# RWKV preparation: TensorE in program order, one tapped projection between keys and receptances, projection parts in front of each key score

## The chip, the cores and the metric

The kernel runs on one core of a Trainium2 chip. The metric is the time of one execution in device microseconds (us). Five engines work side by side, each through its own queue in order: TensorE (PE, matmuls; PEld, its weight loads), VectorE (DVE), ScalarE (ACT), GpSimd (POOL) and the sync engine (SP), which issues DMAs here. ScalarE and GpSimd issue DMAs too.

## What is computed

One layer of a trunk with two token mixers on the same input, 128 context and 1024 latent tokens (T = 1152), width 1024. A single projection `w_in` gives the receptances, keys and values of the RWKV mixer (each 512 wide, 4 blocks of 128 columns), its decay and rate inputs, the query, key, value, output and gate columns of the mLSTM mixer, and the merge gates. The part that matters here, of the RWKV mixer:

```
decay = exp(-DECAY_SCALE * sigmoid(w0 + einsum(tanh(wd), w_up)))      # per direction
a = sigmoid(a0 + einsum(ad, a_up))                                    # per direction
kk = k * kk_scale ;  kk = kk / max(norm(kk, per head), 1e-12)
k_dir = k * (1 + (a - 1) * k_a)
# per token: S = S*w - (S kk)(kk a)^T + v k^T ;  y = S r  (forward and backward)
bonus = sum(r * k_dir * r_k) * v
```

The scan over tokens is worked in chunks of 64 tokens. For a chunk, products of keys with decays (KR, BK) give a 64x64 triangular system for each head; its inverse (the "solve") is made before the scan. The mLSTM queries and keys get a 3x3 convolution over the latent grid ("taps") and SiLU.

## The kernel before

A projection of 128 columns (`gemm_block`, line 389) loads its weights (issued by ScalarE), splits them into a high and a low part (`split_w`, line 353: ScalarE line 367, VectorE line 368), and runs three parts of 384 tokens (`gemm_part`); a part is 24 matmuls (3 products of halves x 8 slices of the depth) into one of three large PSUM buffers, and an evacuation by ScalarE. `zr_block` (line 419) adds the token shift of the RWKV columns (`zr_shift`, four VectorE instructions, lines 414 and 416). `zm_qk` (line 578) is a tapped projection: after its evacuation VectorE runs 10 instructions of `conv_taps` (lines 47 and 50), then SiLU and a write to memory. `zm_o`, `zm_v`, `zm_gates` and `zg` are untapped.

The preparation is the loop of four passes p from line 603, one for two heads each. A pass projects keys (kt), receptances (rt) and values (vt), and makes the norm of the keys: squares, the matmul `ptss` with a block of ones (line 627), its evacuation on VectorE (line 628), Ln and Exp on ScalarE, line 631. Then for each direction d: rate matmuls `ptw` and `pta` (lines 642 and 646) with Sigmoid evacuations into the single tiles cs and at, and three groups g of 6 chunks. A group has a running sum on VectorE (line 653 or 655), two Exp on ScalarE, some nine VectorE instructions that fill the tiles KR and BK (two buffers each), four writes to memory by sync, and the key score `ptA` (line 690, 12 matmuls of 64x64, seen as 24 records), which needs lines 667, 669 or 671, and 677. ScalarE evacuates the score into Am (line 691), and after three groups four DMAs write it to Ad. ptss, ptw, pta, ptA and the transposes share five small PSUM buffers. After both directions come the transposes of the values and the bonus (line 720).

`solve` (line 506) works on an engine of its own choice: it loads Ad, runs 31 steps of two instructions (lines 526 and 528) and writes Xnd and Xtd. GpSimd runs five solves, called in passes 1 to 3; VectorE runs the sixth, at the end of pass 3. The scan behind line 725 loads KR, BK, Xtd (tile TT) and Xnd (tile XN) of its first chunks, and starts with the scores `psc` (line 850) and the merge `pmh`, `pmt` (lines 874 and 883).

The order within each engine is drawn up before the run by a planner, from the program's order, from costs of its own, and from free buffers; an engine can so take a later step early. An instruction issued by an `Ordered` engine while its switch `on` is set keeps program order on that engine. In the preparation no switch was set. FILL (line 598) lists the mLSTM and gate projections that follow each direction's work: the first of a pass stands behind direction 0, the others at the end of the pass, and the planner moved their parts between the scores.

## Time and profile before

| | |
|---|---|
| median of 3 runs | 2254.72 us (2248.45 to 2261.33) |
| the profiled execution | 2242.87 us, span of its instructions 2241.2 us |
| granted TensorE clock, mean | 0.972 |
| busy: PE, DVE, ACT, POOL | 2097.6, 1379.5, 820.4, 566.2 us |
| preparation, first ptss to first psc | 131.94 to 619.18 us |

The trace can be asked in several views: busy time by stretch, groups of instructions by line, the timeline of one engine or of all, and the waits. Times of the trace are microseconds from the span's start. "Idle before" is the engine's time without work just before an instruction, and behind the arrow stands what ended it. A busy TensorE is not TensorE at its peak, as its matmuls overlap; its work is better counted by the distance between starts.

### The profile page before, as it was taken

What the parts mean: (1) busy time and instruction counts of PE and PEld (TensorE: products, weight loads), DVE (VectorE), ACT (ScalarE), POOL (GpSimd) and SP (SyncE); (2) the same over time, 40 slices, a digit from 0 to 9 for tenths busy, and PEclk for the clock granted to TensorE, in tenths of its full rate; (3) what the DMA queues carried; (4) which work ended last, traced back from release to release, by engine and by line L of the source; (5) the groups of instructions that cost most, each with busy time, mean ns of one, the idle gap of its engine ahead of it and who ended that gap; (6) DMA issues with size and microseconds to landing.
All of it is one profiled execution on the core that took longest, in us unless ns stands there. A gap on an engine that the chain in (4) does not pass through costs nothing. (4 is left out here: it accounts for less than half of the span.)

```text
span 2241.2 us, 39749 instructions
## 1 busy us (share of the span) xinstructions
PE 2097.6 (94%) x16323; PEld 1936.2 (86%) x16323; DVE 1379.5 (62%) x2155; ACT 820.4 (37%) x1611; POOL 566.2 (25%) x727
## 2 busy tenths in 40 slices
PE   6999998998889989979889999999999999999996
PEld 4998998988878878878888878999999999999995
DVE  4766777879655566654743465645656665566558
ACT  3664746363134433346421244432221222212213
POOL 2000198888722324255312111000000000000004
PEclk8999999999989999989999999999999999999999
DMA  9134443645645655377676531211111021111104
GB/s 267 54 89 124 117 129 99 164 108 137 167 134 129 158 135 127 109 221 235 193 238 203 183 120 69 67 47 40 55 57 48 29 66 51 51 30 57 47 20 169
DMA packets 382453, 254.55 MB, mean 114 GB/s; under 512 B 86305, under 2 KB 357829, under 8 KB 382272
## 3 DMA queue, kind: packets, MB, share of 16 engines
q1 hardware_dynamic: 235232, 139.11, 22.2%
q10 hardware_dynamic: 136912, 88.56, 13.5%
q0 software_dynamic: 10128, 24.35, 4.0%
q8 instruction: 128, 2.10, 0.4%
q14 instruction: 53, 0.43, 0.1%
HBM read 186.73 MB, written 65.23 MB: 112 GB/s over the span
## 5 line engine op out<-in xcount | busy, mean ns | idle before, releaser
L381 PE MATMUL pg<-act,whi 128*128 128x384 f32 (+1 forms) x3808 | 724.7, 337 | 0.5 <-DVE act L344 0.4
L381 PEld LDWEIGHTS pg<-act,whi 128*128 128x128 f32 (+1 forms) x3808 | 665.9, 188 | 12.8 <-DVE act L344 0.8
L381 PE MATMUL pg<-act,wlo 128*128 128x384 f32 (+1 forms) x1904 | 373.0, 336 | 7.8 <-DVE wlo L368 7.8
L381 PEld LDWEIGHTS pg<-act,wlo 128*128 128x128 f32 (+1 forms) x1904 | 332.8, 187 | 11.3 <-DVE wlo L368 8.1
L368 DVE TENSOR_TENSOR wlo<-wraw,whi 128x1024 fp32r<-128x1024 f32 x130 | 165.0, 1270 | 222.1 <-ACT whi L367 221.9
L47 DVE SCALAR_TENSOR_TENSOR ua<-uraw,par,ua 128x945 f32<-128x945 f32 (+2 forms) x176 | 214.7, 1220 | 39.5 <-ACT ua L1516 36.4
L381 PE MATMUL pfd<-whi,f 128*128 128x512 f32 x792 | 227.5, 395 | 6.5 <-DVE facc L1588 6.5
L1590 POOL TENSOR_TENSOR x<-facc,grow 128x512 f32<-128x512 f32 x17 | 24.3, 1452 | 822.7 <-DVE facc L1588 822.7
L367 ACT ACTIVATE whi<-wraw 128x1024 fp32r<-128x1024 f32 x130 | 136.7, 1053 | 166.8 <-PE pg L381 83.8
L381 PEld LDWEIGHTS pfd<-whi,f 128*128 128x128 f32 x792 | 146.4, 188 | 37.2 <-DVE facc L1588 9.1
L1588 DVE TENSOR_TENSOR facc<-pfd,facc 128x512 f32<-128x512 f32 x180 | 122.0, 686 | 52.3 <-PE pfd L381 52.3
L528 POOL TENSOR_TENSOR Lb<-Lb,tmp 96x31 f32<-96x31 f32 (+15 forms) x155 | 129.7, 837 | 12.1
L526 POOL TENSOR_TENSOR tmp<-La,Lb 96x31 f32<-96x31 f32 (+15 forms) x155 | 120.2, 776 | 28.0 <-DMA La<-Ad 16.2
L381 PE MATMUL pfd<-wlo,f 128*128 128x512 f32 x396 | 122.6, 391 | 0.0
L1520 ACT ACTIVATE ua<-ua 128x1152 f32<-128x1152 f32 x22 | 25.7, 1168 | 217.2 <-DVE ua L47 217.2
L69 PE MATMUL pg<-act,whi 128*128 128x384 f32 x496 | 104.3, 362 | 0.0
L1530 ACT ACTIVATE f<-ua 128x384 fp32r<-128x384 f32 x66 | 32.1, 518 | 194.1 <-DVE ua L1529 194.1
L69 PEld LDWEIGHTS pg<-act,whi 128*128 128x128 f32 x496 | 92.1, 203 | 1.1
L1464 PE MATMUL pwo<-whi,act 128*128 128x512 f32 x288 | 90.2, 393 | 1.1 <-ACT whi L367 1.1
L47 DVE SCALAR_TENSOR_TENSOR qacc<-zraw,par,qacc 128x945 f32<-128x945 f32 (+2 forms) x64 | 84.2, 1316 | 9.7 <-ACT qacc L584 9.2
L381 PEld LDWEIGHTS pfd<-wlo,f 128*128 128x128 f32 x396 | 74.3, 188 | 16.8
L860 DVE TENSOR_TENSOR KA<-psc,msk 64x512 f32<-64x512 f32 x72 | 49.2, 684 | 63.8 <-ACT A L859 58.1
(398 smaller groups left out, 3289.8 us busy)
## 6 DMA issues: line engine op xcount, KB each, us to landing
wraw<-in_w_in ACTq DMA_DIRECT2D x44, 512.0 KB
wraw<-in_ffn_up ACTq DMA_DIRECT2D x44, 512.0 KB
zraw<-in_ada_w SPq DMA_DIRECT2D x24, 512.0 KB
wraw<-in_ffn_down ACTq DMA_DIRECT2D x22, 512.0 KB
KRd<-KR SPq DMA_DIRECT2D x24, 384.0 KB
sgz<-zraw ACTq DMA_DIRECT2D x16, 576.0 KB
KA<-KRd SPq DMA_DIRECT2D x72, 128.0 KB
BKs<-BKd SPq DMA_DIRECT2D x36, 256.0 KB
```

The lines of the kernel that those rows point to most:

```text
L47: v.scalar_tensor_tensor(o, img[:, r0 + i:r1 + i, c0 + j:c1 + j], wt, o, op0=ALU.mult, op1=ALU.add)
L69: return (lambda *a, **k: tc.keep_in_program_order(f(*a, **k))) if self.on else f
L367: s.activation(hi, raw, AF.Copy)
L368: v.tensor_tensor(lo, raw, hi.bitcast(F32), op=ALU.subtract)
L381: pe.matmul(out, wt(hw, k), at(ha, k), start=(i == 0), stop=(i == last))
L526: e.tensor_tensor(t3, L[:, j, i].unsqueeze(2).to_broadcast([NI, n, m]), X[:, j:j + 1, c].to_broadcast([NI, n, m]), op=ALU.mult)
L528: e.tensor_tensor(X[:, i, c], X[:, i, c], t3, op=ALU.subtract)
L860: v.tensor_tensor(q.KA[orr, :, h, :], sc_[h][orr], msk[orr, d:d + 1, :].to_broadcast([64, 4, 128]), op=ALU.mult)
L1464: pe.matmul(pts[b][q], AS[g][:, ha, k, 128 * o:128 * o + 128], wo2[k][hw][:, 0, 512 * q:512 * q + 512], start=(k == 0 and i == 0), stop=(k ...
L1520: s.activation(ua, ua, AF.Silu)
L1530: s.activation(f2[:, 0, gs], ua[:, gs], AF.Copy)
L1588: v.tensor_tensor(acc[:, b, qs], pt, acc[:, b, qs], op=ALU.add)
```

## The change

TensorE's switch is set for the preparation, so its instructions keep the program's order there. A projection becomes a generator that stops after each part (a "step"). A pass now projects keys, then one tapped projection, then receptances; the values and the rest of FILL form a chain of steps, and two, two, two, one, two and one of them are issued in front of the six key scores, the others at the end of the pass. The rates of direction 1 are issued behind the first of the two steps in front of direction 0's last score. FILL is reordered so that a tapped projection comes first in each pass. Three small steps of each group go from VectorE to ScalarE: the copies to WL, the copy of the first column of KR, and the scale and bias of kx. The calls of the other fill functions turn into `yield from` in the same manner as the one shown.

```diff
@@ -386,10 +387,16 @@
         mm_split(pt[:ncol], lambda h, k: w2[h][:, k, :], lambda h, k: AS[g][:, h, k, :], nk)
         evac(g, pt)
 
-    def gemm_block(src, evac, nk=8, ncol=128, ps_=None):
+    def gemm_steps(src, evac, nk=8, ncol=128, ps_=None):
+
         w2 = split_w([kp(src)], nk, ncol)
         for g in range(3):
             gemm_part(w2, g, evac, ncol, nk, ps_)
+            yield
+
+    def gemm_block(*a, **k):
+        for _ in gemm_steps(*a, **k):
+            pass
 
     w_in = A["w_in"][0]
 
@@ -416,10 +423,14 @@
             v.scalar_tensor_tensor(dst[:, a:b - 1], raw[:, a + 1:b], hmu[:, i:i + 1], dst[:, a:b - 1],
                                    op0=ALU.mult, op1=ALU.add)
 
+    def zr_steps(i, dst):
+        raw = stage()
+        yield from gemm_steps(w_in[:, 128 * i:128 * i + 128], zr_evac(i, raw, dst))
+        zr_shift(i, raw, dst)
+
     def zr_block(i, dst):
-        raw = stage()
-        gemm_block(w_in[:, 128 * i:128 * i + 128], zr_evac(i, raw, dst))
-        zr_shift(i, raw, dst)
+        for _ in zr_steps(i, dst):
+            pass
 
 
     rows = [mods1(0)]
@@ -565,7 +576,7 @@
 
         def evac(g, pt):
             s.activation(vf[:, G3 * g:G3 * g + G3], pt, AF.Copy)
-        gemm_block(w_in[:, 2944 + 128 * f:3072 + 128 * f], evac)
+        yield from gemm_steps(w_in[:, 2944 + 128 * f:3072 + 128 * f], evac)
         vs = stage()
         for q in range(3):
             pt = pss([128, 3, 128], "ptvm")
@@ -595,11 +606,12 @@
             return [(slice(0, 2), slice(0, 2), -1), (slice(14, 18), slice(2, 6), -1)]
         return [(slice(14 - 6 * g + 0, 20 - 6 * g), slice(0, 6), -1)]
 
-    FILL = [[(zm_o, 0), (zm_qk, 0), (zm_gates, 0), (zm_qk, 1)],
-            [(zm_o, 1), (zm_qk, 2), (zm_v, 0), (zm_qk, 3)],
-            [(zm_o, 2), (zm_qk, 4), (zm_v, 1), (zm_qk, 5)],
-            [(zm_o, 3), (zm_qk, 6), (zm_v, 2), (zm_qk, 7), (zm_v, 3), (zg, 0), (zg, 1), (zg, 2),
-             (zg, 3)]]
+
+    FILL = [[(zm_qk, 0), (zm_o, 0), (zm_gates, 0), (zm_qk, 1)],
+            [(zm_qk, 2), (zm_o, 1), (zm_v, 0), (zm_qk, 3)],
+            [(zm_qk, 4), (zm_o, 2), (zm_v, 1), (zm_qk, 5)],
+            [(zm_qk, 6), (zm_o, 3), (zm_v, 2), (zm_v, 3), (zm_qk, 7), (zg, 0), (zg, 1), (zg, 2), (zg, 3)]]
+    pe.on = True
     for p in range(4):
         pc = slice(128 * p, 128 * p + 128)
         wraw = stage()[:, 0:512]
@@ -613,10 +625,13 @@
         v.tensor_tensor(wup[1], wraw, wup[0].bitcast(F32), op=ALU.subtract)
         kt = pp.tile([128, T], F32, name="kt", tag="kt")
         zr_block(4 + p, kt)
+        fn, f = FILL[p][0]
+        for _ in fn(f):
+            pass
         rt = pp.tile([128, T], F32, name="rt", tag="rt")
         zr_block(p, rt)
         vt = pp.tile([128, T], F32, name="vt", tag="vt")
-        zr_block(8 + p, vt)
+        steps = chain(zr_steps(8 + p, vt), *(fn(f) for fn, f in FILL[p][1:]))
 
         kk = pp.tile([128, T], F32, name="kk", tag="kk")
         sq = pp.tile([128, T], F32, name="sqk", tag="zmisc")
@@ -631,8 +646,7 @@
         v.scalar_tensor_tensor(kk, kt, P("rwkv_kk_scale", p), kk, op0=ALU.mult, op1=ALU.mult)
         kds = pp.tile([128, T], F32, name="kds", tag="kds")
         rf = rst.rearrange("p c t -> p (c t)")
-        for d in range(2):
-            Am = pp.tile([128, NCH, LC], F32, name="Am", tag="zmisc")
+        def rates(d):
             cs_ = pp.tile([128, T], F32, name="cs", tag="cs")
             at_ = pp.tile([128, T], F32, name="at", tag="at")
             for g in range(3):
@@ -645,6 +659,11 @@
                 for i in range(2):
                     pe.matmul(pt, wup[i][:, 2 + d], zad[d][:, gs], start=(i == 0), stop=(i == 1))
                 s.activation(at_[:, gs], pt, AF.Sigmoid, bias=P("rwkv_a0", 4 * d + p))
+            return cs_, at_
+
+        for d in range(2):
+            cs_, at_ = rates(0) if d == 0 else nxt
+            Am = pp.tile([128, NCH, LC], F32, name="Am", tag="zmisc")
             for g in range(3):
                 gs = slice(G3 * g, G3 * g + G3)
                 cg = slice(6 * g, 6 * g + 6)
@@ -662,16 +681,16 @@
                 e0 = LC - 1 if d == 0 else 0
                 f0 = 0 if d == 0 else LC - 1
                 for n, c, st in wl_pos(d, g):
-                    v.tensor_copy(WL[:, n, d, p:p + 1] if st is None else WL[:, n, d, p:p + 1][:, ::st],
-                                  KR[:, c, 1, e0:e0 + 1])
-                v.tensor_copy(KR[:, :, 0, f0:f0 + 1], kk3[:, :, f0:f0 + 1])
+                    s.activation(WL[:, n, d, p:p + 1] if st is None else WL[:, n, d, p:p + 1][:, ::st],
+                                 KR[:, c, 1, e0:e0 + 1], AF.Copy)
+                s.activation(KR[:, :, 0, f0:f0 + 1], kk3[:, :, f0:f0 + 1], AF.Copy)
                 if d == 0:
                     v.tensor_tensor(KR[:, :, 0, 1:LC], kk3[:, :, 1:LC], KR[:, :, 1, 0:LC - 1], op=ALU.mult)
                 else:
                     v.tensor_tensor(KR[:, :, 0, 0:LC - 1], kk3[:, :, 0:LC - 1], KR[:, :, 1, 1:LC], op=ALU.mult)
                 v.tensor_tensor(KR[:, :, 1, :], KR[:, :, 1, :], r3, op=ALU.mult)
                 kx = kd if d == 0 else BK[:, :, 1, :]
-                v.tensor_scalar(kx, at, P("rwkv_k_a", p), oka[:, p:p + 1], op0=ALU.mult, op1=ALU.add)
+                s.activation(kx, at, AF.Identity, scale=P("rwkv_k_a", p), bias=oka[:, p:p + 1])
                 v.tensor_tensor(kx, kx, k3, op=ALU.mult)
                 v.tensor_tensor(BK[:, :, 0, :], at, kk3, op=ALU.mult)
                 v.tensor_tensor(BK[:, :, 0, :], BK[:, :, 0, :], cs, op=ALU.mult)
@@ -683,6 +702,11 @@
                 for x in range(2):
                     dma(BKd[d, cg, p, 64:128, 64 * x:64 * x + 64].rearrange("c k n -> k c n"),
                         BK[64:128, :, 1 - x, :])
+                next(steps)
+                if (d, g) == (0, 2):
+                    nxt = rates(1)
+                if (d, g) not in ((1, 0), (1, 2)):
+                    next(steps)
                 pt = pss([128, 6, LC], "ptA")
                 for c in range(6):
                     for h in range(2):
@@ -698,10 +722,6 @@
                 solve(2, d, v, pp.tile([128, T], F32, name="Lb", tag="kk"))
             elif p > 0:
                 solve(p - 1, d, gp)
-            if d == 0:
-                fill = iter(FILL[p])
-                fn, f = next(fill)
-                fn(f)
 
         vst = pp.tile([128, NB, 128], F32, name="vst", tag="zmisc")
         for q in range(3):
@@ -720,8 +740,9 @@
             pe.matmul(pt, blk, kds[:, gs], start=True, stop=True)
             v.tensor_tensor(vt[:, gs], pt, vt[:, gs], op=ALU.mult)
         dma(bond[p], vt)
-        for fn, f in fill:
-            fn(f)
+        for _ in steps:
+            pass
+    pe.on = False
     stp.close()
     if stop in ("prep", "sol"):
         return
```

## Rows read from the trace of the kernel before

**Rows 1.** The page, section 1: busy time of each engine, its share of the span, and instructions.

```profile
PE 2097.6 (94%) x16323; PEld 1936.2 (86%) x16323; DVE 1379.5 (62%) x2155; ACT 820.4 (37%) x1611; POOL 566.2 (25%) x727
```

**Rows 2.** Busy time by stretch (windows), one stretch for each pass of the preparation from its first ptss to the next, the last one to the first psc. Columns: from:to, length, busy us of PE, PEld, DVE, ACT and POOL with their instructions, granted TensorE clock, DMA share, GB/s.

```profile
131.90:236.40 104.50, 103.22 (x695) 93.43 (x694) 70.14 (x113) 56.43 (x91) 0.00 (x0) 1.00 0.45 114
236.40:345.40 109.00, 104.69 (x704) 99.98 (x703) 80.93 (x113) 61.55 (x96) 62.98 (x74) 1.00 0.51 133
345.40:462.60 117.20, 109.58 (x705) 104.89 (x704) 94.38 (x113) 61.86 (x96) 101.85 (x129) 0.94 0.46 120
462.60:619.20 156.60, 136.47 (x858) 130.38 (x857) 124.94 (x172) 60.98 (x96) 121.55 (x165) 0.96 0.57 148
```

**Rows 3.** The same columns for the stretch from ptss to the end of the bonus matmuls, of pass 2 and of pass 3.

```profile
345.40:411.20 65.80, 58.18 (x406) 53.71 (x405) 61.46 (x84) 38.76 (x58) 55.29 (x70) 0.90 0.52 130
...
462.60:532.90 70.30, 57.96 (x413) 53.01 (x412) 65.88 (x86) 39.37 (x59) 57.95 (x74) 0.95 0.52 135
```

**Rows 4.** The timeline of all engines late in pass 3 (start us, length, engine, line, operation, tiles, count).

```profile
610.77 2.93 PE L381 MATMUL pg<-act,whi 128*128 128x384 f32 x16
...
614.93 2.93 PE L381 MATMUL pg<-act,whi 128*128 128x384 f32 x16
```

**Rows 5.** Groups of instructions by line over 95 to 610 us: count | busy us, mean ns of one | idle time of the engine just before them, and what ended it.

```profile
L381 PE MATMUL pg<-act,wlo 128*128 128x384 f32 (+1 forms) x772 | 154.1, 338 | 7.8 <-DVE wlo L368 7.8
...
L47 DVE SCALAR_TENSOR_TENSOR qacc<-zraw,par,qacc 128x945 f32<-128x945 f32 (+2 forms) x64 | 84.2, 1316 | 9.7 <-ACT qacc L584 9.2
...
L690 PE MATMUL ptA<-KR,BK 64*64 64x64 f32 x576 | 24.2, 236 | 21.5 <-DVE BK L677 21.4
...
L584 ACT ACTIVATE qacc<-pg,par 128x384 f32<-128x384 f32 x24 | 13.7, 578 | 6.3 <-DMA qkd<-qacc 6.3
...
L414 DVE SCALAR_TENSOR_TENSOR rt<-zraw,hmu,rt 128x127 f32<-128x127 f32 (+1 forms) x8 | 7.5, 935 | 2.8 <-ACT rt L409 2.7
```

**Rows 6.** TensorE's timeline in short windows at the first ptss and the first key score (ptA) of passes 0 to 3, and at the third key score of pass 1. A window's end cuts the count and the length. In brackets: idle time before, and what ended it.

```profile
131.94 1.45 PE L627 MATMUL ptss<-sqk,blk 128*128 128x384 f32 x4
...
146.75 0.92 PE L690 MATMUL ptA<-KR,BK 64*64 64x64 f32 x24 [1.18 <-DVE BK L677]
...
236.45 1.45 PE L627 MATMUL ptss<-sqk,blk 128*128 128x384 f32 x4
...
253.87 0.85 PE L690 MATMUL ptA<-KR,BK 64*64 64x64 f32 x21 [0.65 <-DVE BK L677]
...
263.08 0.73 PE L690 MATMUL ptA<-KR,BK 64*64 64x64 f32 x17 [0.79 <-DVE BK L677]
...
345.47 1.77 PE L627 MATMUL ptss<-sqk,blk 128*128 128x384 f32 x5
...
366.24 1.01 PE L690 MATMUL ptA<-KR,BK 64*64 64x64 f32 x14 [4.01 <-DVE BK L677]
...
462.60 1.13 PE L627 MATMUL ptss<-sqk,blk 128*128 128x384 f32 x3
...
484.60 0.56 PE L690 MATMUL ptA<-KR,BK 64*64 64x64 f32 x12 [1.42 <-DVE BK L677]
```

**Rows 7.** VectorE's groups by line: the conv taps between ptss and bonus of pass 2 (first two rows), and the steps that the change moves, over passes 1 to 3 (the other four).

```profile
L47 DVE SCALAR_TENSOR_TENSOR qacc<-zraw,par,qacc 128x945 f32<-128x945 f32 (+2 forms) x6 | 7.3, 1224 | 0.0
L50 DVE SCALAR_TENSOR_TENSOR qacc<-zraw,par,qacc 128x127 f32<-128x127 f32 x2 | 1.4, 691 | 0.0
...
L665 DVE COPY WL<-KR 128x6 f32<-128x6 f32 (+2 forms) x21 | 7.9, 460 | 3.3 <-ACT KR L660 3.3
L667 DVE COPY KR<-kk 128x6 f32<-128x6 f32 x18 | 7.1, 393 | 2.4 <-DMA KRd<-KR 2.3
L674 DVE TENSOR_SCALAR BK<-at,par,oka 128x384 f32<-128x384 f32 x9 | 5.3, 589 | 0.0
L674 DVE TENSOR_SCALAR kds<-at,par,oka 128x384 f32<-128x384 f32 x9 | 4.8, 536 | 1.5 <-ACT at L647 1.5
```

**Rows 8.** The timeline where the preparation meets the scan: GpSimd's first scan memsets, sync's loads of TT, TensorE's first score and merge, and a small ScalarE copy.

```profile
596.07 2.71 POOL L780 MEMSET AB<- 64x256 f32 x8 [5.80 <-DMA Xnd<-Lb]
...
599.63 2.31 SPq L75 DMA_DIRECT2D TT<-Xtd  x4
...
605.71 2.37 SPq L75 DMA_DIRECT2D TT<-Xtd  x4
...
619.18 1.16 PE L850 MATMUL psc<-KA,BKs 64*128 64x128 f32 x16
...
630.08 0.88 PE L883 MATMUL pmt<-TT,HT 32*32 32x32 f32 x32 [0.38 <-ACT HT L876]
...
629.75 0.28 ACT L876 ACTIVATE HT<-pmh 128x128 f32<-128x128 f32 x1 [0.99 <-PE pmh L874]
```

**Rows 9.** GpSimd's timeline at the start of the first solve and the end of the fifth, and (last two rows) the stretches of the second and the third solve, with the columns of rows 2.

```profile
271.40 0.53 POOL L515 DMA_DIRECT2D La<-Ad  x1 [185.74 <-DMA Ad<-Am]
...
275.13 0.36 POOL L526 TENSOR_TENSOR tmp<-La,Lb 96x31 f32<-96x31 f32 x1 [2.03 <-DMA La<-Ad]
...
589.76 0.51 POOL L531 DMA_DIRECT2D Xtd<-La  x1 [0.29 <-POOL La L530]
...
339.70:400.80 61.10, 53.79 (x365) 50.56 (x364) 51.12 (x67) 38.74 (x58) 52.32 (x68) 0.89 0.46 112
400.80:465.80 65.00, 64.29 (x384) 61.71 (x382) 46.49 (x47) 28.10 (x46) 54.62 (x69) 1.00 0.48 132
```

More of the change, by code (lines that the diff above doesn't have):

```diff
@@ L1 @@
 from contextlib import ExitStack
+from itertools import chain
 import numpy as np
@@ L541, in evac @@
             s.activation(sg[:, G3 * g:G3 * g + G3], pt, AF.Tanh, scale=0.5)
-        gemm_block(w_in[:, 3984 + 128 * f:4112 + 128 * f], evac, ps_=ps_)
+        yield from gemm_steps(w_in[:, 3984 + 128 * f:4112 + 128 * f], evac, ps_=ps_)
         adma(sgz[f], sg)
@@ L551, in evac @@
             s.activation(gt[:16, G3 * g:G3 * g + G3], pt[:16], AF.Identity, bias=gb)
-        gemm_block(w_in[:, 3968:3984], evac, ncol=16)
+        yield from gemm_steps(w_in[:, 3968:3984], evac, ncol=16)
         adma(gtd, gt[:16])
@@ L559, in evac @@
             s.activation(so[:, G3 * g:G3 * g + G3], pt, AF.Sigmoid)
-        gemm_block(w_in[:, 3456 + 128 * f:3584 + 128 * f], evac)
+        yield from gemm_steps(w_in[:, 3456 + 128 * f:3584 + 128 * f], evac)
         adma(sod[:, :, f, :].rearrange("b p t -> p b t"), so.rearrange("p (b t) -> p b t", t=128))
@@ L584, in evac @@
             s.activation(acc[:, G3 * g:G3 * g + G3], pt, AF.Copy, scale=P("mlstm_conv", 8 * 4 + f))
-        gemm_block(w_in[:, 1920 + 128 * f:2048 + 128 * f], evac)
+        yield from gemm_steps(w_in[:, 1920 + 128 * f:2048 + 128 * f], evac)
         conv_taps(v, raw, acc, lambda t: P("mlstm_conv", 8 * t + f))
```

## The prediction

> **What bounds the kernel now.** I read the page first: TensorE is busy 94% of the span [rows 1]. That figure counts pipelined matmuls and says little about a single stage, so I looked at the stretches of the stage that the diff touches. The preparation runs from the first head-norm matmul (ptss, line 627) at 131.94 to the first scan score (psc, line 850) at 619.18 [rows 6, 8]. Cut at the ptss of each of the four passes p, it takes 104.5, 109.0, 117.2 and 156.6 us; TensorE is idle 33.3 of these 487.3 us, and in the last two passes its granted clock was 0.94 and 0.96 of full, a mean between its levels of 1.2 and 2.4 GHz [rows 2], some 13 us more (0.06 x 117.2 + 0.04 x 156.6).
>
> How much of the 487.3 is work? One third of a projection ("a part": 24 matmuls) costs 4.16 us when nothing waits, from one 16-matmul row to the next [rows 4]. 30 projections lie in the stretch: 90 parts, 374.4 us. Each pass adds six ptss and six bonus records (line 720) at 0.32 us, the difference between a row of four and a row of three [rows 6], so 3.9; 24 rate matmuls at 4.16 / 24, 4.2; six key scores (ptA, line 690) at 0.92 [rows 6], 5.5; nine transposes, about 1 by an estimate from their 128 columns against 384. That is 14.6, times four 58.4, and 4 for the values' transposes. Sum 436.8: **50.5 us are lost**. This is the most that an order of TensorE can give.
>
> Who takes them? In the line groups the key scores wait 21.5 us, all but a tenth for line 677 on VectorE, and one part waits 7.8 us for its low weights, line 368 [rows 5]. From ptss to the bonus, VectorE is busy 61.5 of 65.8 us in pass 2 and 65.9 of 70.3 in pass 3 [rows 3]: there it is the bound, and the conv taps that the planner puts in between (7.3 + 1.4 us in pass 2) are part of it [rows 7].
>
> A second chain is as long. GpSimd's five solves run back to back from 271.40, when the first one's load is issued, to 589.76, when the last Xtd is written: 318.4 us [rows 9]. They start when both directions' scores of pass 0 and then the first direction of pass 1 are there, and the scan needs the last one. At 596 the scan's buffers come free and its loads start [rows 8]. TensorE still has parts until 619.18, so this end is hidden today.
>
> **The change part by part.** *TensorE's order.* Per pass it is now fixed: key projection, tapped projection, receptance, ptss, rates of direction 0, then two, two and two parts in front of the key scores of direction 0, one, two and one in front of those of direction 1. The rates of direction 1 go before the last two-part gap's second part. The work stays 436.8.
>
> *The first key score* is what ends late. It now has 1.9 (ptss) + 2.1 (rates) + 2 x 4.16 = 12.3 us of cover after the first ptss. In the trace it started 14.8, 17.4, 20.8 and 22.0 us after it, each time after a wait for line 677 [rows 6], so these are the times at which its operands were ready. Unchanged, they cost 2.5 + 5.1 + 8.5 + 9.7 = 25.8 us: the upper end. VectorE is relieved, though. The taps of the first projection now run beside receptance (12.5 us of cover for 84.2 / 8 = 10.5 us of line 47 [rows 5] and 1 to 1.4 of line 50 [rows 7]), those of the last behind the scores; and three steps of each group go to ScalarE, 25.1 us in three passes or 8.4 each [rows 7]. About three kx, two first-column and two WL copies lay ahead of the first score, some 3.4 us at these means. Against that, the receptance's shift and the last taps now lie ahead of line 628 on VectorE, and with five small PSUM buffers the third rate matmul waits for the first line 628, with nothing else allowed on TensorE. I take waits of 2, 3.5, 6 and 6, 17.5 in all; the lower end, all relief and no new queue, is 8.
>
> *The other scores* have 9 us between them and the first of direction 1 has 2.1 + 4.16 + 0.92 + 4.16 = 11.3 from its rates; I take 1 us a pass for these and for the bonus, which has only the transposes in front (4 in all, bounds 0 and 10). The tail of pass 3 keeps a wait like the 7.8 us one, as the VectorE solve still competes with line 368: 5, bounds 2 and 8. Low clock behind such waits: 5, bounds 2 and 13, the loss by [rows 2]. Sum 31.5 instead of 50.5. **TensorE ends the preparation at 131.9 + 436.8 + 31.5 = 600**, bounds 581 and 626.
>
> *The moved steps on ScalarE.* A scaled 384-column pass takes 0.58 us there (line 584, [rows 5]); for six columns no row exists. The nearest, 128 columns, is 0.28 [rows 8], the other end is 0 if it fills idle time; I take 0.2. Per pass that is 6 x 0.58 + 13 x 0.2 = 6 us, on an engine that is busy 61 to 62 us of 109 to 117 [rows 2]. It is hidden unless ScalarE's queue holds a score's evacuation, a wait on TensorE, in front of them; that belongs to the bounds above. DMA queues gain nothing; sync's writes of a group move with it.
>
> *The solves.* The third score of pass 1 now comes 1.9 + 2.1 + 5 x 4.16 + 2 x 0.92 + 2.1 + 4.16 = 33 us after ptss and the 3.5 of waits, 36.5; before it was 26.6 [rows 6]. Pass 0 gets 0.5 longer than 104.5 by the same sums. The first solve so starts 10.4 us later, at 281.8. At the same pace the last Xtd goes out at 600.2. How much GpSimd gains by VectorE's relief has no row: between 0 and the 25.1 us moved. The five solve slots speak for the low end: the third had least VectorE work, 46.5 us, and still took 65.0, the second had 51.1 and took 61.1 [rows 9]. I take 3: **the last Xtd at 597**.
>
> The Trainium skill ("SBUF — State Buffer", section "SBUF: two separate sides") says that VectorE and GpSimd hold their common SBUF ports one at a time, the loser waiting out the whole instruction. By that rule all of the moved time could come back to GpSimd, the last Xtd would go out at 575 and TensorE would set the scan's start; by the slots above I give it little, and it stands as a rival.
>
> *The scan's start.* The pacing step is the merge matmul pmt, at 630.08. Its last input, the second direction's TT, was issued from 605.71 for 2.37 us [rows 8]; with 3.7 us from issue to use, as the first solve's load took [rows 9], pmt could have run at 611.8. Now the last Xtd lands at about 597 + 0.5 + 3.7 = 601.2 instead of the release at 596.0: the loads move by 1.6 (against the first TT load, 599.63) to 5.2 us. pmt at 613.4 to 617, I take 615.5. TensorE's own side gives 600 + 10.9 (619.18 to 630.08) = 611, so **the solves, not TensorE, now end last**. The gain is 630.1 - 615.5 = 14.6 us, less 0.6 for a first scan score at TensorE's low level (an estimate, half of its 1.16 us [rows 8]): 14 us. Most of the 19 us won in TensorE's order turn into its waiting for GpSimd. Everything behind the scan's start is unchanged and follows it.
>
> The profiled execution took 2242.87 us; 14 less is 2228.9. It lies 11.9 below the median of the runs shown, 2254.72, and that median is what I predict against: **2240.7**.
>
> **The rivals.** (1) *Fixed waits.* The scores' operands come as late as before and TensorE, which can't slip in other parts, pays 25.8 us at the first scores and some of each other bound; it ends at 610 to 625, pmt at 621 to 636, the time between 9 less and 6 more, about 2252. For it: pass 2 and 3 wait 4.0 and 1.4 us even now with more cover. Against: VectorE's load between ptss and bonus falls from 61.5 to about 48 in pass 2 (less 8.7 of taps and 8.4 of moved steps, plus receptance's shift, 3.7 as twice line 414 [rows 5]). An order that changes nothing in effect would land here too. (2) *Slower: the taps hold up the head norm.* VectorE works its queue in order; if the taps start late (their evacuation waited 6.3 us for the earlier result's write [rows 5]) they and the receptance's shift stand before line 628, and rates, parts and scores wait behind it. It decides from a first line 628 more than 9 us behind ptss: 8 us more in each of passes 1 to 3, and some 3 each of low clock (13 us spread over the four longest waits), so that TensorE ends at 633 and pmt comes at 644: 14 us slower, 2268.7. (3) *GpSimd gets free.* With 25 us off the solves TensorE's end sets the start: pmt at 611, 19 us less, 2236 with the cold start.
>
> **How the numbers follow.** Forecast 0.47 (8 to 19 us less), rival 1 0.27, rival 2 0.16, rival 3 0.10. A measurement tells about 0.5%, 11 us, from no change. Four fifths of the forecast and all of rival 3 lie beyond it: faster 0.48; the rest of the forecast and rival 1: same 0.36; slower 0.16. The range goes from 24 us less, where solves and waits both take their better ends (2231), to 7 more (2262), where it leaves out most of rival 2.
>
> **What would show it.** Right: psc behind an idle stretch of TensorE of some 8 to 12 us; the first solve's load near 282 and the last Xtd near 597; first key scores 14 to 18 us after ptss; VectorE under 56 us busy between ptss and bonus in pass 2. Wrong: no idle stretch before psc (rival 1 or 2; a late line 628 tells the second), or the last Xtd before 585 (rival 3). The prediction falls if the planner orders VectorE and ScalarE otherwise than I assume, since only TensorE's order is fixed.

## The result and the profile after

The changed kernel took 2277.54 us (median of 4 runs, 2274.86 to 2279.77); the kernel before took 2252.65 in the same comparison. The ratio is 1.0103, 95% interval 1.0081 to 1.0124: 25 us slower, where 14 us less had been forecast. The profiled execution took 2276.15 us. Page, section 1, of the changed kernel [rows 1]:

```profile
PE 2099.9 (92%) x16323; PEld 1938.0 (85%) x16323; DVE 1364.8 (60%) x2079; ACT 836.2 (37%) x1687; POOL 561.9 (25%) x727
```

Work is moved, not saved; what grew is idle time. The four passes, cut as in [rows 2]:

```profile
131.90:241.90 110.00, 104.94 (x696) 94.92 (x695) 67.74 (x93) 64.17 (x113) 0.00 (x0) 0.98 0.43 108
241.90:352.80 110.90, 106.13 (x704) 101.45 (x703) 75.28 (x93) 65.13 (x115) 50.10 (x62) 0.98 0.47 122
352.80:463.70 110.90, 107.11 (x703) 101.97 (x702) 92.34 (x92) 64.37 (x114) 95.66 (x115) 0.97 0.52 136
463.70:637.10 173.40, 137.74 (x859) 130.99 (x857) 114.44 (x150) 62.70 (x112) 136.72 (x191) 0.89 0.49 130
```

Passes 0 and 1 are 7.4 us longer than before (220.9 against 213.5) and pass 2 is 6.3 shorter (110.9 against 117.2), so that the three together seem to cost 1.1 us only. Pass 3 is 16.8 us longer, at a granted clock of 0.89 instead of 0.96. TensorE is idle 49.3 of 505.2 us (before 33.3 of 487.3), 35.7 of them in pass 3 (before 20.1).

TensorE's line groups of the changed kernel, 131 to 640 us (count | busy, mean ns | idle before, and what ended it; an instruction issued under the switch shows line 70):

```profile
L70 PE MATMUL pg<-act,whi 128*128 128x384 f32 (+1 forms) x1440 | 276.8, 345 | 11.7 <-ACT zraw L552 10.1 <-ACT qacc L595 1.6
L70 PE MATMUL pg<-act,wlo 128*128 128x384 f32 (+1 forms) x727 | 142.2, 337 | 19.3 <-DVE wlo L369 19.3
L70 PE MATMUL ptA<-KR,BK 64*64 64x64 f32 x576 | 22.2, 224 | 4.5 <-DVE BK L696 4.5
L70 PE MATMUL ptw<-twd,wup 128*128 128x384 f32 x48 | 13.9, 370 | 2.9 <-DVE kk L643 2.8
L70 PE MATMUL pta<-zad,wup 128*128 128x384 f32 x48 | 13.7, 367 | 10.5 <-ACT cs L657 10.5
```

The key scores' wait has gone from 21.5 [rows 5] to 4.5 us: the steps in front of them cover. Grown are the waits of the rate matmuls (ptw and pta, 13.4 us instead of 1.8 before), which want a free small PSUM buffer, and those of the projection parts, 31 us instead of 7.8. Nearly all of the 31 lie in the tail of pass 3 (TensorE's timeline):

```profile
587.69 2.93 PE L70 MATMUL pg<-act,wlo 128*128 128x384 f32 x8 [19.30 <-DVE wlo L369]
...
603.18 5.18 PE L70 MATMUL pg<-act,whi 128*128 128x384 f32 x16 [8.25 <-ACT zraw L552]
...
618.65 3.05 PE L70 MATMUL pg<-act,whi 128*128 128x384 f32 x16 [0.59 <-ACT zraw L552]
...
624.38 3.06 PE L70 MATMUL pg<-act,whi 128*128 128x384 f32 x16 [1.28 <-ACT zraw L552]
...
637.08 1.16 PE L871 MATMUL psc<-KA,BKs 64*128 64x128 f32 x16
```

Who is late? VectorE's timeline shows it idle, then in its solve; ScalarE's shows a SiLU (line 598) waiting for taps that stand among the last steps of that solve, and gate evacuations (line 552), which would free TensorE's PSUM, behind the SiLU:

```profile
555.07 0.19 DVE L537 TENSOR_TENSOR tmp<-La,Lb 96x31 f32<-96x31 f32 x1 [14.52 <-POOL tmp L537]
```
```profile
564.26 1.06 ACT L368 ACTIVATE whi<-wraw 128x1024 fp32r<-128x1024 f32 x1 [2.28 <-PE pg L70]
600.29 1.28 ACT L598 ACT_TABLE_LOAD   x1 [34.97 <-DVE qacc L48]
601.58 1.16 ACT L598 ACTIVATE qacc<-qacc 128x1152 f32<-128x1152 f32 x1
602.65 0.47 ACT L552 ACTIVATE zraw<-pg 128x384 f32<-128x384 f32 x1
```

The weights' high half is copied at 564.26, and its low half should follow on VectorE a microsecond later; TensorE gets it at 587.69. VectorE's solve waited 14.52 us because its load went out only at 551.05: its tile is one of three that GpSimd's solves use too. That chain started late, as GpSimd's and sync's timelines show [rows 9]:

```profile
295.05 0.53 POOL L526 DMA_DIRECT2D La<-Ad  x1 [209.39 <-DMA KRd<-KR]
...
547.73 0.51 POOL L542 DMA_DIRECT2D Xtd<-La  x1 [0.29 <-DMA vmd<-zraw]
...
605.99 1.04 POOL L542 DMA_DIRECT2D Xtd<-La  x1 [0.29 <-POOL La L541]
614.73 2.71 POOL L801 MEMSET AB<- 64x256 f32 x8 [7.70 <-DMA Xtd<-La]
```
```profile
285.28 5.15 SPq L76 DMA_DIRECT2D Ad<-Am  x4
...
551.05 0.32 SPq L76 DMA_DIRECT2D La<-Ad  x1
```

The first solve is loaded at 295.05 (before 271.40), the last Xtd written at 605.99 (before 589.76). The merge comes at 652.43 instead of 630.08, 22.3 us later: 17.9 by the end of TensorE's parts and 4.4 between the first score and the merge. That is most of the 25 us between the medians. (The profiled pair differs by 33 us at the end: from pmt on, the profiled executions of the kernels below took 1611 to 1629 us in no order that their starts explain, and the one of before, 1611, is the shortest.)

### The profile page after: what moved, and what is told of

Read it like the earlier page. It is cut to its first block, busy times and chain, and to the rows that moved or that the text cites. A ratio compares the mean times of both kernels' runs of the same rounds, so it can differ in the third digit from the quotient of the medians.

```text
span 2274.3 us, 39828 instructions
## 1 busy us (share of the span) xinstructions
PE 2099.9 (92%) x16323; PEld 1938.0 (85%) x16323; DVE 1364.8 (60%) x2079; ACT 836.2 (37%) x1687; POOL 561.9 (25%) x727
## 5 line engine op out<-in xcount | busy, mean ns | idle before, releaser
L382 PE MATMUL pg<-act,whi 128*128 128x384 f32 x2224 | 418.7, 335 | 0.5 <-DVE act L345 0.4
L70 PE MATMUL pg<-act,whi 128*128 128x384 f32 (+1 forms) x2080 | 406.1, 347 | 11.7 <-ACT zraw L552 10.1
L382 PEld LDWEIGHTS pg<-act,whi 128*128 128x128 f32 x2224 | 388.6, 188 | 7.2 <-DVE act L345 0.7
L70 PEld LDWEIGHTS pg<-act,whi 128*128 128x128 f32 (+1 forms) x2080 | 370.3, 193 | 20.4 <-ACT zraw L552 11.1
L70 PE MATMUL pg<-act,wlo 128*128 128x384 f32 (+1 forms) x1040 | 203.4, 337 | 19.3 <-DVE wlo L369 19.3
L382 PE MATMUL pg<-act,wlo 128*128 128x384 f32 x1112 | 215.2, 334 | 0.0
L70 PEld LDWEIGHTS pg<-act,wlo 128*128 128x128 f32 (+1 forms) x1040 | 182.3, 188 | 21.5 <-DVE wlo L369 19.6
L382 PEld LDWEIGHTS pg<-act,wlo 128*128 128x128 f32 x1112 | 194.8, 188 | 0.0
L539 POOL TENSOR_TENSOR Lb<-Lb,tmp 96x31 f32<-96x31 f32 (+15 forms) x155 | 122.5, 790 | 12.2
```

The costliest lines, as they stand in the source:

```text
L70: return (lambda *a, **k: tc.keep_in_program_order(f(*a, **k))) if self.on else f
L382: pe.matmul(out, wt(hw, k), at(ha, k), start=(i == 0), stop=(i == last))
L539: e.tensor_tensor(X[:, i, c], X[:, i, c], t3, op=ALU.subtract)
```

## The experiments

Each ratio is to the kernel before on the same chip. That kernel took 2252.4 to 2255.2 us (medians) in these comparisons, so a difference of 2 or 3 us between two runs says nothing. Places in the profile are those of the one profiled execution of each kernel.

**Is it the late solve in VectorE's queue?** `own_load` gives that solve's load a tile of its own, `early_solve` has one part fewer in front of each score of pass 1, direction 0, and `no_order` drops TensorE's switch. `moves_back` puts the three moved steps back on VectorE.

```diff
-        Lf = sp.tile([NI, 1024], F32, name="La", tag="L", bufs=3)      # own_load
+        Lf = sp.tile(...) if spare2 is None else spare2[:NI, :1024]    # spare2: tile "La", tag "at"
-                next(steps)                                            # early_solve
+                if (p, d) != (1, 0):
+                    next(steps)
-    pe.on = True                                                       # no_order
```

> The changed kernel, but VectorE's solve loads Ad into the tile that held the rates (at), not into one of the three L buffers that GpSimd's solves hold. Late-solve theory (GpSimd's solves start 23.6 us later, so the fourth still holds the buffers; VectorE stands behind its own load from 540.6 to 555.1, and TensorE behind VectorE): the load goes out near 537 instead of 551, the 19.5 us wait for low weights shrinks below 8, psc comes at 615 to 625 instead of 637, time about 2262. Fixed-order rival (TensorE's program order itself costs, wherever VectorE stands): psc stays within 5 us of 637 and the time within 5 us of 2277.5.

Measured: 2270.04 us, ratio 1.0082 (1.0059 to 1.0104), 7.5 us less than the changed kernel. VectorE's load goes out at 534.2, and the wait for wlo shrinks from 19.30 to 2.92. Then ScalarE is next. TensorE's timeline:

```profile
573.01 2.93 PE L70 MATMUL pg<-act,wlo 128*128 128x384 f32 x8 [2.92 <-DVE wlo L369]
590.13 5.49 PE L70 MATMUL pg<-act,whi 128*128 128x384 f32 x16 [8.50 <-ACT zraw L552]
618.42 5.35 PE L70 MATMUL pg<-act,whi 128*128 128x384 f32 x16 [8.61 <-ACT zraw L552]
```

The first score comes at 633.4, and neither expectation held in full. The shared tile is one cause, worth about a third.

> The changed kernel with one part less in front of each key score of pass 1, direction 0 (one, one, one; the three go to the end of the pass). Late-solve theory: the first solve starts about 12 us earlier than 295, the fourth is out near 536 instead of 548, VectorE's solve waits about 3 us and not 14.5, psc near 622, time 2260 to 2265; pass 1 itself gets up to 5 us longer at its key scores. Fixed-order rival: the scores of pass 1 have less cover, so the time is 2277 to 2285.

Measured: 2272.02, ratio 1.0092 (1.0071 to 1.0114), 5.5 us less. That lies between the two expectations. The first solve is loaded at 281.1, 14 us sooner, but the first score of pass 1 then waits 8.7 us and pass 2 begins 8.5 us later. Pass 3, where no part was moved, is 16.5 us shorter all the same (156.9 from ptss to psc instead of 173.4): there the late solves had cost. What the cover gives and what the solves lose are traded one for the other.

> The changed kernel with the three small steps of each group back on VectorE. Late-solve theory: they are off the path that sets the end; VectorE gets 30 us more in the stage, the first key scores come up to 4 us later in passes 2 and 3, time 2275 to 2290. ScalarE rival (ScalarE in its order holds up the scores' evacuation, and so the writes of Ad and the first solve): the first solve starts 5 or more us earlier and the time is 2265 or less.

Measured: 2283.39, ratio 1.0147 (1.012 to 1.0175): in this order the moved steps save some 6 us.

> The changed kernel without the switch that keeps TensorE in program order; the program's order, the fill list and the moved steps stay. Fixed-order rival: the planner slips parts into the waits again, so the time is that of the kernel before, 2247 to 2260. Late-solve theory: the time follows the first solve's start; if the planner lets the scores of pass 1 come near 263 to 270 as before, the time is below 2262, and if the first solve's load stays behind 290, it is 2270 or more though the order is free.

Measured: 2253.19 (10 runs), ratio 1.0007 (0.9992 to 1.0021). **The fixed order costs 24 us; with the order free, all else in the change together does nothing that can be measured.** TensorE now reaches the first psc at 609.50, 9.7 us sooner than in the kernel before, and gets nothing for it. Timelines of TensorE and ScalarE:

```profile
609.50 1.16 PE L870 MATMUL psc<-KA,BKs 64*128 64x128 f32 x16
...
626.14 2.66 PE L870 MATMUL psc<-KA,BKs 64*128 64x128 f32 x16 [14.90 <-ACT BT L885]
...
631.80 0.88 PE L903 MATMUL pmt<-TT,HT 32*32 32x32 f32 x32 [0.38 <-ACT HT L896]
```
```profile
596.91 0.49 ACT L552 ACTIVATE zraw<-pg 128x384 f32<-128x384 f32 x1 [0.32 <-PE pg L382]
615.94 0.38 ACTq L360 DMA_DIRECT2D wraw<-in_w_in  x1
618.13 0.34 ACTq L554 DMA_DIRECT2D sgz<-zraw  x1
618.52 0.87 ACT L552 ACTIVATE zraw<-pg 128x384 f32<-128x384 f32 x2 [21.12 <-DMA KA<-KRd]
```

The scan's second score waits 14.90 us for ScalarE (BT), which stands in order behind the issue of a weight load, at 615.94, and the last gate evacuations, 18.5 us after its last piece of work. In the kernel before, ScalarE was no sooner (first row: the same evacuations; then the first score's, there and in no_order):

```profile
618.49 0.87 ACT L541 ACTIVATE zraw<-pg 128x384 f32<-128x384 f32 x2 [9.83 <-DMA KA<-KRd]
...
623.49 0.56 ACT L859 ACTIVATE A<-psc 32x128 f32<-32x128 f32 x2 [0.86 <-ACT zraw L541]
```
```profile
624.91 0.56 ACT L879 ACTIVATE A<-psc 32x128 f32<-32x128 f32 x2 [1.49 <-DMA TT<-Xtd]
```

So ScalarE's queue held the scan's start to about the same time in both kernels, though TensorE came 9.7 us sooner in one.

**Where in the preparation does the order cost?** `front_free` sets the switch from pass 2 on, `pass3_free` in passes 0 to 2, `tail_free` until the bonus of pass 3.

```diff
-    pe.on = True            # front_free and pass3_free
     for p in range(4):
+        pe.on = p > 1       # front_free;  p < 3 in pass3_free
...
         dma(bond[p], vt)
+        pe.on = p < 3       # tail_free
```

> The changed kernel with TensorE's order free in passes 0 and 1 and fixed in passes 2 and 3. Freeing pass 3 gave 8 of the 24 us, so the other 16 should lie here if the late first solve (loaded at 295) is what the order of passes 0 and 1 costs: first La near 280, GpSimd's fourth solve done by 535, VectorE's load near 538, 2256 to 2264. If the order of pass 2 or the shape of the whole matters instead: 2270 to 2278.

> The changed kernel with TensorE's order fixed in passes 0 to 2 and free in all of pass 3. Tail theory: little more than the free tail gives, since the four waits ahead of the first key score of pass 3 cost about 6 us: 2250 to 2260. Rival, passes 0 to 2 cost: 2266 to 2275, because the first solve of the chain is loaded at 295 as in the changed kernel.

> The changed kernel with TensorE's program order given up only behind the bonus of pass 3 (the trailing steps of that pass); passes 0 to 2 and the front of pass 3 stay fixed. Tail theory (the fixed order costs because TensorE stands in its tail behind one step whose operand VectorE and ScalarE deliver late, 19.5 + 8.4 us, while other steps are ready): first psc at 612 to 622 instead of 637, time 2253 to 2262. Rival, the order costs in every pass and through the late first solve: the solve chain still begins at 295 and ends at 606, first pmt not before 640, time 2268 to 2275.

Measured: front_free 2265.16, ratio 1.0057 (1.0029 to 1.0084); pass3_free 2269.79, 1.0072 (1.0055 to 1.0088); tail_free 2268.51, 1.0068 (1.0051 to 1.0085). Freeing passes 0 and 1 gives 12.4 us, freeing pass 3 7.8, its tail alone 9.0. My tail theory is refuted as the whole story: a free tail still waits for wlo (groups of TensorE, 131 to 640 us, tail_free). VectorE made the low half after that one at 600.98 only, so no other projection had both halves of its weights.

```profile
L382 PE MATMUL pg<-act,wlo 128*128 128x384 f32 x136 | 28.0, 348 | 16.6 <-DVE wlo L369 16.6
```

Freeing passes 0 and 1 gives at least as much as freeing pass 3 (the intervals overlap). These two become 8.2 us shorter (212.7 instead of 220.9), about what they had lost; pass 2 stays at 110.9. The first solve is loaded at 278.6 and VectorE's at 538.6, 12.4 sooner, but the tail still has its two waits (16.0 and 7.5 us): pass 3 begins 8 us sooner and is 3.7 us shorter. So the order of the early passes costs mostly in these passes themselves; the shorter pass 2 hid that in the sum.

**What do the parts of the change do on the kernel before?** `before_order` adds the switch alone, `before_moves` the moved steps alone.

> The kernel before with the order switch alone: its own program order, no tap reordered, no step moved. If the fixed order costs whatever the program order is, by the loss of 24 us that freeing the changed kernel showed: about 2275. If the steps put in front of the key scores carry what they were put there for, the order without them is far dearer: in each of four passes the first key scores come about 18 us behind ptss with some 6 us of work between, and the same for direction 1 in part, so 12 to 25 us a pass, 48 to 100 in all: 2300 to 2350.

Measured: 2357.69, ratio 1.0463 (1.0435 to 1.0491), 104 us slower. The groups of TensorE say why:

```profile
L69 PE MATMUL ptA<-KR,BK 64*64 64x64 f32 x576 | 36.7, 315 | 126.9 <-DVE BK L678 121.4 <-DVE KR L668 5.5
```

That is above even the dearer of the two ranges. With nothing in front of them the scores wait 126.9 us, in the changed kernel 4.5. The steps in front of the scores do what they are for: with the rest of the change they buy back 80 of these 104 us, and no more.

> The kernel before with the three moved steps alone (the copies into WL and KR and the scaling into kx on ScalarE instead of VectorE). In the changed kernel they were worth 6 us (2283.4 with them on VectorE, 2277.5 without). If VectorE's load delays the solves here too: 2245 to 2250. If the scan's start is held by ScalarE's queue and the scan's own loads: 2251 to 2256.

Measured: 2280.53, ratio 1.0131 (1.0103 to 1.0158): 26 us slower, where I had expected none or a gain. VectorE's groups, 350 to 540 us, of this kernel and (second fence) of the kernel before:

```profile
L368 DVE TENSOR_TENSOR wlo<-wraw,whi 128x1024 fp32r<-128x1024 f32 x8 | 10.6, 1331 | 30.8 <-ACT whi L367 30.8
```
```profile
L368 DVE TENSOR_TENSOR wlo<-wraw,whi 128x1024 fp32r<-128x1024 f32 x10 | 17.7, 1772 | 7.9 <-ACT whi L367 7.9
```

VectorE has less to do and waits 30.8 us instead of 7.9 for ScalarE's copy of the high half. The planner drew up another order for ScalarE; which of its shifts does it was not tried. So the same three steps are worth -6 us in one order and +26 in another.

**Does the rest add up?** `own_early` joins own_load and early_solve, `own_early_tail` adds tail_free to them, `untapped_first` restores FILL of before (which also puts the last tapped projection back in front of zm_v 3 in the tail), `untapped_own_tail` joins it with own_load and tail_free.

> The changed kernel, order fixed, with the load buffer of its own for VectorE's solve and with one part fewer in front of each key score of pass 1, direction 0. Late-solve theory: the two gains (7.5 and 5.5 us) add only in part, because both act on when VectorE's solve is loaded; what stays is ScalarE's queue behind the SiLU: 2264 to 2270. If they add up: 2264.5 or less.

> The changed kernel with all three named causes taken away: a load buffer of its own for VectorE's solve, one part fewer ahead of the key scores of pass 1, direction 0, and TensorE's order given up behind the bonus of pass 3. If these are the whole of the 24 us that the fixed order costs: 2252 to 2258, first psc 612 to 618. If something else in the fixed passes costs as well: 2260 to 2268.

Measured: 2270.96, ratio 1.0076 (1.0052 to 1.01), and 2264.72, 1.005 (1.003 to 1.0069). The gains don't add: 6.6 us for two that gave 7.5 and 5.5, and 12.8 for all three. Some 11 of the 24 us stay, in the fixed passes; they were not split further.

> The changed kernel with the order of the mLSTM projections as before: the untapped zm_o stands between keys and receptances, the first tapped zm_qk among the steps in front of the key scores. If the taps in front of the head norm hold up line 628 (the prediction's second rival), undoing this gives time back: 2262 to 2272. If the tapped projection there does what the forecast said (its taps run beside the receptance projection), undoing it puts 10.5 us of taps a pass beside the scores' operands on VectorE, and the first or second key score comes some 5 us later in each pass: 2282 to 2300.

Measured: 2268.95, ratio 1.0062 (1.0042 to 1.0082), 8.6 us less. The number fits the first case, the trace doesn't. The last two passes (columns as in the windows above):

```profile
351.30:471.80 120.50, 108.93 (x703) 103.48 (x702) 91.39 (x94) 61.73 (x112) 99.35 (x125) 0.96 0.47 121
471.80:626.40 154.60, 136.57 (x856) 130.02 (x855) 125.66 (x157) 57.85 (x110) 127.22 (x171) 0.96 0.52 138
```

Pass 2 is 9.6 us longer without the tapped projection in front, as my second case had it, but passes 0 and 1 are 1.5 us shorter, and pass 3 is 18.8 us shorter: in its tail the SiLU waits 10.1 us instead of 34.97. So the tapped projection between keys and receptances helps pass 2 alone, and what else the edit of FILL does costs more. The new order zm_v 3, zm_qk 7 at the end may be it; it was not tried apart. The first solve is also loaded 8 us sooner here (286.8).

> The changed kernel, steps in front of the key scores still fixed, with the untapped projection between keys and receptances, a load buffer of its own for VectorE's solve, and TensorE's order given up behind the bonus of pass 3. Alone these gave 8.6, 7.5 and 9.0 us. If they add up: 2252 to 2256. If they overlap, since all three act on when VectorE's solve and the last parts can run: 2258 to 2266.

Measured: 2270.63, ratio 1.0071 (1.0043 to 1.0099). That is above both ranges, and no better than untapped_first alone. Its VectorE load goes out at 559.1, later than the 553.1 there, so the tile of its own bought nothing.

**With the order free, what holds the scan's start?** `free_own_load` and `untapped_free` are no_order with own_load and with FILL of before; `free_no_stores` leaves out the four stores of sgz in pass 3 and stores zeros ahead of pass 0; `free_one_less` and `before_one_less` move gate block 3 into the scan (NZ0 = 3).

> The changed kernel without the fixed order and with a buffer of its own for the load of VectorE's solve. If the start of the scan is set by the solves, an earlier VectorE solve (loaded at 520 instead of 538) brings the last Xtd to about 580 and the time to 2243 to 2249. If it is set by TensorE's second psc behind ScalarE's in-order evacuations of the sgz steps, the time stays at 2250 to 2256.

> The changed kernel without the fixed order and with the mLSTM projections in the order of before. If the tapped projection costs only where TensorE can't go on with other parts: no difference to the free kernel with taps, 2250 to 2257. If it costs by itself, through VectorE's queue ahead of the first key scores: 2243 to 2248.

> The changed kernel without the fixed order, and with the four stores of sgz in pass 3 left out (zeros of the same size are stored ahead of pass 0, so gate blocks 0 to 3 are not the reference's). If the DMA engines and ScalarE's queue hold the start of the scan, it comes 8 to 15 us sooner: second psc by 615, time 2238 to 2246. If something else holds it (the solves, the loads of the scan): 2249 to 2256.

> The changed kernel without the fixed order and with gate block 3 moved from pass 3 into the scan, so 12.5 us less of TensorE and one store less ahead of the scan. If TensorE's work still sets the start: 12 us sooner at the start, some of it paid in the scan: 2241 to 2250. If the release of the buffers and the DMA engines set it: the store less gives 2 to 4 us, and the scan pays for the block: 2250 to 2262.

> The kernel before with gate block 3 moved from pass 3 into the scan. By the prediction, TensorE's work sets the scan's start here (release 596, first psc 619), so the start should come up to 12 us sooner: 2241 to 2249. If the DMA engines hold the second psc: 2250 to 2260.

| | us | ratio, interval | psc, pmt |
|---|---|---|---|
| no_order | 2253.19 | 1.0007, 0.9992 to 1.0021 | 609.5, 631.8 |
| free_own_load | 2254.6 | 1.0006, 0.9993 to 1.002 | 612.1, 628.9 |
| untapped_free | 2253.01 | 1.0002, 0.9988 to 1.0017 | 612.9, 630.5 |
| free_no_stores | 2252.77 | 0.9995, 0.9973 to 1.0017 | 610.1, 625.9 |
| free_one_less | 2258.75 | 1.0023, 1.0003 to 1.0044 | 608.9, 624.4 |
| before_one_less | 2263.23 | 1.0039, 1.0022 to 1.0056 | 607.1, 625.4 |

TensorE can be done 6 to 12 us sooner than in the kernel before, and the merge moves by 6 us at most. In `free_own_load` VectorE's load goes out at 537.5, as in no_order (537.8) and not at the 520 that I expected, so this run says nothing of the solves. Taking the four stores of 576 KB away brings the merge 6 us forward in the profile, less than the 8 to 15 expected, and the times don't show it. With one block less the start comes 5 to 7 us sooner and the block is paid later: from the last pmt on, 1328 and 1329 us, against 1309 to 1321 in all the other kernels. While the free kernel waits, the DMA engines are full (windows of no_order; the last two columns are DMA share and GB/s):

```profile
610.00:615.00 5.00, 1.25 (x16) 0.89 (x13) 0.00 (x0) 0.00 (x0) 3.70 (x7) 0.82 1.07 212
615.00:620.00 5.00, 0.00 (x0) 0.00 (x0) 0.00 (x0) 0.87 (x2) 0.00 (x0) 0.50 1.15 216
620.00:625.00 5.00, 0.00 (x0) 0.00 (x0) 1.23 (x1) 1.52 (x3) 0.00 (x0) 0.50 1.06 264
```

That the scan's loads, the stores and ScalarE's DMA issues crowd there is shown, and that the second score waits for ScalarE; what holds ScalarE's issue back was not taken apart.

No version beat the kernel before.

## Why the prediction was wrong, step by step

**TensorE ends at 600.** It ended at 637.1, so 68.4 us were lost over the 436.8 of work instead of 31.5. By the terms of the sum:

| term | forecast | measured |
|---|---|---|
| ptss to first score, and other scores | 17.5 + 4 | 17.9 (ptw 2.9, pta 10.5, ptA 4.5) |
| tail of pass 3 | 5 (2 to 8) | 29.4 (19.30 + 8.25 + 0.59 + 1.28) |
| other idle time | none | 2.0 (49.3 less the above) |
| lost while busy ("low clock") | 5 (2 to 13) | 19.1 (68.4 - 49.3) |

The size of the first term is luck in part. Of its 17.9 us, 4.5 are the scores' own wait, in pass 1, and 2.9 the wait that the forecast named, the third rate's for VectorE's line 628 (now 643), in pass 3. The other 10.5 are those of the last rate (pta) in passes 0, 2 and 3: it wants the buffer of the first rate, whose Sigmoid stands behind the norm's Ln in ScalarE's queue. In pass 0:

```profile
136.62 1.16 ACT L644 ACTIVATE kk<-kk 128x1152 f32<-128x1152 f32 x1
...
139.10 0.58 ACT L657 ACTIVATE cs<-ptw,par 128x384 f32<-128x384 f32 x1
...
139.73 0.62 PE L70 MATMUL pta<-zad,wup 128*128 128x384 f32 x2 [3.95 <-ACT cs L657]
```

After such a wait the scores find their operands. The first ones started 18.2, 17.4, 19.0 and 21.0 us after ptss, for a forecast of 14 to 18 (the third row is the third score of pass 1):

```profile
150.18 0.92 PE L70 MATMUL ptA<-KR,BK 64*64 64x64 f32 x24
...
259.23 1.20 PE L70 MATMUL ptA<-KR,BK 64*64 64x64 f32 x24 [4.54 <-DVE BK L696]
...
281.59 0.92 PE L70 MATMUL ptA<-KR,BK 64*64 64x64 f32 x24
...
371.74 0.92 PE L70 MATMUL ptA<-KR,BK 64*64 64x64 f32 x24
...
484.74 0.92 PE L70 MATMUL ptA<-KR,BK 64*64 64x64 f32 x24
```

**The step that failed is "the tail of pass 3 keeps a wait like the 7.8 us one".** It was put at 5 us and measured 29.4. I took the wait of a planner's order, in which TensorE goes on with another part, for that of a fixed one, and didn't follow the late solve into VectorE's queue, nor the taps behind it into ScalarE's. The last term was wrong by arithmetic of mine: of the 50.5 us lost before, 17.2 were not idle time (50.5 - 33.3), and I let 12 of them vanish with the waits. They go with the mean granted clock of these stretches: 11.4 in no_order (475.4 long, 27.2 idle, clock 0.98), 17.2 before (0.97), 19.1 after (0.95), 31.1 in before_order (598.0 long, 130.1 idle, 0.86).

**The first solve 10.4 us later, at 281.8.** It was 23.6 later. The third score of pass 1 came at 281.59, not 273, and from it to the load it took 13.5 us, not 8.3. The first write of Ad went out 3.7 us after the score, about as before (3.3); but the four took 5.15 us to issue, and before they took 2.46:

```profile
266.34 2.46 SPq L75 DMA_DIRECT2D Ad<-Am  x4
```

From the last of them to the load it took 4.6 us instead of 2.6. Why these steps took longer was not tried; I carried the old 8.3 along.

**The solves gain 3 us from VectorE's relief.** They took 310.9 us instead of 318.4, a gain of 7.4 of the 25.1 moved: rival 3 falls. **VectorE under 56 us busy between ptss and bonus of pass 2** is wrong too: 59.64 of 62.4 us, at 63 instructions instead of 84 (before 61.46, [rows 3]). The 45 instructions with which both kernels fill the groups' tiles took 41.9 us there, and 35.9 before. One of them, same operation and shape, in the changed kernel (352.8 to 415.2) and in the kernel before (345.4 to 411.2):

```profile
L690 DVE TENSOR_TENSOR KR<-kk,KR 128x378 f32<-128x378 f32 x3 | 2.9, 960 | 0.0
```
```profile
L671 DVE TENSOR_TENSOR KR<-kk,KR 128x378 f32<-128x378 f32 x3 | 1.8, 600 | 0.0
```

So some of what VectorE gave up went into its own longer instructions. GpSimd was busy 55.85 of those 62.4 us (before 55.29 of 65.8). The Trainium skill's rule that the two hold their common ports one at a time ("SBUF — State Buffer", "SBUF: two separate sides") would fit this direction. No run took GpSimd away there, so the cause is not shown.

**The moved steps on ScalarE** took 0.70 us (forecast 0.58) and 0.20 us (0.2), so their prices nearly held; that they are hidden holds in this order alone (before_moves).

**The solves set the scan's start, pmt at 615.5.** In the changed kernel TensorE set it: psc follows its last part at once, 22 us after the scan's buffers came free (614.7), and the forecast's idle 8 to 12 us before psc did not come. From psc to pmt it took 15.4 us instead of 10.9, as the second score waited 7.95 us for ScalarE. The other half, that pmt could run at 611.8, is not borne out either: in three kernels without the order, TensorE was done at 609 to 613 and the buffers were free by 599.3, and pmt came at 629 to 632. The forecast had left out ScalarE's evacuations in front of the scan, which stood at 618.5 in the kernel before as well. None of these kernels had the 14 us of gain to give.

**The rivals.** The time passed even rival 2 (2268.7). Its mechanism did not happen (the first line 628 came 1.0, 0.8, 2.3 and 5.0 us after ptss, not over 9). Rival 1 had the right reason, that TensorE can't slip in other parts, but named the scores where the tail paid.

## What to carry to other kernels

When an engine's order is fixed, each wait left in it must be covered by what was put in front of it; so follow every late operand to the end of the stage, through all in-order queues behind it, and not only to the place that the change aims at. A delay early in one chain (a solve 24 us late in pass 1) can be paid two passes later on another engine, so the stretch that got longer need not be the one in which the cost arose, and a sum over several stretches can hide one that lost: look at each, free the order stretch by stretch and measure. And before a gain is put down, free the resource that should give it and see whether the next stage starts sooner: here TensorE's 50 us of loss covered a start that something else held.

## What had not been expected of the hardware

Three VectorE steps moved to ScalarE were worth -6 us in one order and +26 us in the other, at the same prices for each instruction (0.70 and 0.20 us). In the windows above one of VectorE's instructions took 600 ns in one kernel and 960 in the other, at the same shape. And an 8.25 us wait of TensorE in the tail, the second there, cost more than its length: the clock granted from 600 to 605 us was 0.50, the lower of its two levels (1.2 GHz), and the 16 matmuls behind the wait took 5.18 us instead of 2.93.
